# A list scheduler that plans a port: new instruction spacings, the SBUF port of VectorE and GpSimd as a resource, and new stream priorities in a two-layer hybrid backbone

## The chip, the cores and the metric

The kernel runs on one core of a Trainium2 chip. The metric is the device time of one execution in microseconds; the runs of a kernel are told by their median.

## The reference

The model takes 512 latent tokens of 1024 channels and 256 context tokens and runs two layers. Each is an RMSNorm with a learned modulation, a mixer, and a gated residual. The first layer mixes by a convolution of 31 taps and by windowed attention with 16 query heads over 4 key heads; the second by a convolution of 3 taps between gates.

```python
# layer 0
h = xn @ w_in
a = conformer_conv(h[..., :D_CONV], h[..., D_CONV:EV_Q], ...)   # GLU, 31 taps, layer norm, SiLU
q, k = axial_rope(...), axial_rope(...)
att = latent_window_attention(q, k, v, kc, vc, ev_sink[e])      # window of +-128 tokens, 256 context keys, a sink
y = (concatenate([a, att]) * silu(h[..., EV_G:])) @ ev_w_out[e]
x = x + gt * y
# layer 1
bg, cg, u, z = split(xn @ od_w_in[o], 4)
x = x + gt * ((bg * depthwise_conv(cg * u, conv_w, conv_b) * silu(z)) @ w_out)
# end
return rms_norm(x, final_g)
```

All operands are float32. The kernel multiplies each as a high and a low part, three matmuls for one.

## The kernel before

The code does not issue its instructions as it meets them. It records them in a `Plan` (`add`, line 219), gives each a rough duration (`cost`, line 266), and `schedule` (line 311) then orders them by a list schedule: it walks through a modelled time, and whichever engine is free first takes, of its instructions whose operands are ready, the one with the smallest priority number. `issue` (line 441) hands them to the engines in order of their modelled start. That order is fixed in the program; on the chip each engine works through its own list and waits by semaphore for others. As everything is issued in `issue`, nearly all rows of the profile name line 445; one goes by the names of the tiles.

A priority is the place in which an instruction was recorded plus the bias of its stream: `FILL_BIAS` for the eight input projections of the convolution, `Q_BIAS` for queries, `GATE_BIAS` for gates, `CONV_BIAS` for the taps, `ADA_BIAS` for the second layer's modulation, and so on. An instruction becomes ready when its operands' modelled ends plus a spacing from `LATENCY` (line 77, by the two engines) have passed. Some work can go to either of two engines, and `release`, within `schedule`, chooses the one that would end it earlier, with a handicap in ns: `SHY` for VectorE against GpSimd on splits, gates and additions (the engine called `F`), and `NORM_SHY` for ScalarE against VectorE on the normalisation of a row of probabilities (tile p). `LOOK` and `SOON` let a long instruction wait for a more urgent one that will soon be ready; `SWAP_COST` keeps ScalarE from changing its function table too readily.

What the groups of instructions are, by tile:
- Startup: VectorE multiplies rows of the modulation weights by the condition and sums them (junk in silb and ada, 128x1024); GpSimd makes low parts (wsl, xl); TensorE gathers keys, first queries and values.
- Attention, for each of 4 groups of heads and 4 blocks of 128 queries: scores s on TensorE, row maxima mx, the exponent's bias nm and the sink es on VectorE, exponentials p on ScalarE with their sum den, den's reciprocal, p scaled by it on ScalarE or VectorE, p transposed on TensorE (pt), split into th (ScalarE) and tl (VectorE), and the product with the values (po).
- Convolution, next to the attention: six of eight tiles on VectorE, 30 multiply-adds each into a PSUM accumulator (cv); two tiles as products on ScalarE (pr) and sums on GpSimd (cp).
- Weights: each chunk is loaded by SyncE, its high part is made on ScalarE (names ending in h), its low part on GpSimd or VectorE (l).
- The layer norm over channels (tiles u, lnq, lnrdg and others), the output projection (pya, pyb), the second layer's input (x, sq, yh, yl), sixteen blocks of four projections (pcg, pu, pbg, pz), and the last projection (f).

Of the kernel before, what the change touches and what calls it, by code (L numbers as in the profile page):

```python
# [37 lines left out]
SHY = {"DVE": 3000.0}  # L38
HI_SHY = {"POOL": 1000.0}
NORM_SHY = {"ACT": -500.0}  # L40
HI_TAGS = ()
LOOK = 0.2
SOON = 50
SWAP_COST = 800
K1_BIAS = 3.5
Q_BIAS = (0, 2.5, 3.5, 4.5)
FILL_BIAS = (-1, -1, 1, 2, 3, 4, 5, 6)
GATE_BIAS = (4.5, 6.5, 8.5, 10, 10)
# [13 lines left out]
CONV_BIAS = 20  # L62
# [5 lines left out]
for _n, _w in (("g0", 8), ("g1", 8), ("sh0", 8), ("sc0", 8), ("gt0", 8),  # L68
# [8 lines left out]
LATENCY = {"PE": {"*": 196, "PE": 0}, "ACT": {"*": 142, "PE": 271, "POOL": 170}, "DVE": {"*": 128, "PE": 300, "POOL": 155},  # L77
           "POOL": {"*": 130, "PE": 309}, "SP": {"*": 0}}
# [3 lines left out]
class Phases:  # L82
    """Memory that one phase of the kernel after another cuts into tiles of its own."""
# [17 lines left out]
class LTile:  # L101
    """A tile that is allocated when the first instruction that touches it is issued."""
# [24 lines left out]
class View:  # L127
# [12 lines left out]
    def cut(self, n):  # L140
        """free columns (n w) seen as n rows of w."""
        return View(self.t, self.chain + [lambda x: x.rearrange("p (h d) -> p h d", h=n)], self.p0, self.p1,
                    self.ix.reshape(n, -1), self.dtype)
# [17 lines left out]
class Op:  # L161
    __slots__ = ("eng", "dur", "fn", "a", "k", "prio", "deps", "tiles", "succ", "need", "ready", "aset", "seq", "start", "end", "nbytes", "alts", "shy")


class Plan:
    """Records instructions, orders them per engine by a list schedule over rough instruction costs, and
    issues them in that order."""
# [20 lines left out]
    def either(self, *engines):  # L188
        """an engine that is chosen when the operands are ready, by what each has to do until then."""
        plan = self  # L190

        class Rec:
            def __getattr__(self, m):
                return lambda *a, **k: plan.add(engines, m, {n: getattr(x, m) for n, x in engines}, a, k)

        return Rec()

    def pick(self, shy, *forms):
        """one of several (engine, its object, method, arguments, keywords) with the same operands."""
        e, x, m, a, k = forms[0]  # L200
        op = self.add("*", m, None, a, k, forms)
        op.shy = shy
        return op
# [8 lines left out]
    @contextmanager  # L212
    def after(self, *ops):
        """what the block records is ordered behind these instructions."""
        old, self.extra = self.extra, self.extra + list(ops)
        yield
        self.extra = old

    def add(self, eng, m, fn, a, k, forms=None):
# [26 lines left out]
        if isinstance(eng, tuple):  # L246
            op.alts = {}
            for n, _ in eng:
                op.eng = n
                self.cost(op, m, out, outs, a, k)  # L250
                op.alts[n] = (op.dur, fn[n], a, k, None)
            op.eng = "*"
            op.shy = self.shy
        elif forms:
            op.alts = {}
            for n, x, m, a, k in forms:
                op.eng = n
                self.cost(op, m, out, outs, a, k)
                op.alts[n] = (op.dur, getattr(x, m), a, k, op.aset)
            op.eng, op.aset = "*", None  # L260
        else:
            self.cost(op, m, out, outs, a, k)
# [3 lines left out]
    def cost(self, op, m, out, outs, a, k):  # L266
        if op.eng == "SP":
            v = out if isinstance(out, View) else k["in_"]
            op.nbytes = v.n * 4 * (v.p1 - v.p0)
            op.dur = 60  # L270
            return
# [5 lines left out]
        if op.eng == "PE":  # L277
            rhs = k.get("rhs")
            if m == "transpose":
                op.dur = n * 2 / 2.4  # L280
            elif rhs is not None and rhs.dtype == F32R:
                op.dur = n / 2.4 * (1 if n >= 256 else 4)
            elif rhs is not None and rhs.dtype == BF16:
                op.dur = n / 2.4
            else:
                op.dur = max(4 * n / 2.4, COLUMN)
# [24 lines left out]
    def schedule(self):  # L311
# [4 lines left out]
        dma_free, aset = 0.0, None  # L316

        def release(op):
            if op.alts:
# [7 lines left out]
                op.dur, op.fn, op.a, op.k, op.aset = best[2]  # L327
# [11 lines left out]
        while len(order) < total:  # L339
# [16 lines left out]
            pick, back = None, []  # L356
            while avail[e]:
# [15 lines left out]
                if e == "ACT" and op.aset and op.aset != aset and pick is None and avail[e]:  # L373
                    # another table: let ready work that needs no change go first unless this is far ahead
# [5 lines left out]
                    break  # L380
                pick = op
                break
            if pick is None and back:
                pick = self.ops[back.pop(0)[1]]
# [4 lines left out]
            if pick.dur > 300 and pend[e]:  # L389
                # a more urgent instruction that is ready in a moment goes first  # L390
# [15 lines left out]
            for t in op.tiles:  # L406
                if t not in alloc:
# [3 lines left out]
                    for pr, s in waiting.pop(t.key, []):  # L411
                        heapq.heappush(pend[self.ops[s].eng], (now, pr, s))
            op.start = now
            free[e] = now + dur
            op.end = now + dur
            if e == "SP":
                dma_free = max(dma_free, now + 1000) + op.nbytes / 360.0
                op.end = dma_free + 1000
            order.append(op)
            for t in op.tiles:  # L420
                t.left -= 1
                t.free_at = max(t.free_at, op.end)
                if not t.left:
# [6 lines left out]
                    for pr, s in more:  # L430
                        heapq.heappush(pend[self.ops[s].eng], (t.free_at + 200, pr, s))
            lat = LATENCY[e]
            for s in op.succ:
                s.need -= 1
                s.ready = max(s.ready, op.end + lat.get(s.eng, lat["*"]))
# [13 lines left out]
def backbone_kernel(ctx, tc, x_d, ctx_d, xT_d, c_d, cols_d, ada0_d, ada1_d, ws_d, wi0_d, woa_d, woc_d, wi1_d, wo1_d,  # L449
# [18 lines left out]
    # three banks: values at first, scores next, then accumulators of one bank each  # L468
# [54 lines left out]
    # mlo keeps key >= query, mhi keeps key <= query  # L523
# [4 lines left out]
    # 1 + bias of the scale columns of both layers  # L528
# [16 lines left out]
    def load_w(src, name, lo_eng, tag=None):  # L545
        """a chunk's high and low parts, each as halves of 512 columns."""
# [30 lines left out]
    # row 0 of the identity without its one, as 128 zeros  # L577
    zero, some = ident[0:1].bitcast(BF16)[:, 2:2 + P], ones[0:1].bitcast(BF16)

    def clear(bank_):  # L580
        """opens the accumulation of several groups in one bank."""
# [8 lines left out]
    def rstd_bcast(sums, n, dst, name):  # L590
        """1/sqrt(mean+eps) on every partition, from means with the tokens on partitions."""
# [11 lines left out]
    def weigh(tile_, sil_, acc, junk, eng, scale=1.0):  # L603
        """acc = scale * sum over the free axis of tile_ * sil_."""
# [6 lines left out]
    # ================= layer 0 =================  # L611
# [17 lines left out]
    def normed(t, name):  # L629
        """a block of tokens (on partitions) over its root mean square."""  # L630
# [20 lines left out]
    # keys, the first queries and the values accumulate while the modulation of each input tile arrives  # L651
# [25 lines left out]
    def modulated(k, e, src):  # L677
        """an input tile, its channels on partitions."""
# [80 lines left out]
    # keys: rows 0:64 and 64:128 both hold the head, high parts in KH, low parts in KL  # L759
    KH, KL, KC = [None] * NKV, [None] * NKV, [None] * NKV  # L760

    def twice(out, h, src):
        """(high, low) parts of one head's rows of src; the rows that hold it, and the others."""
# [23 lines left out]
    def query(pq, name):  # L787
        """the rotated queries of two heads: even head as [high; low] rows, odd head as [low; high]."""
# [19 lines left out]
    # values: per key block and head [high | low]  # L808
# [21 lines left out]
    # sigmoid(v) = (1 + tanh(v/2))/2, its half within the weights of the taps  # L830
# [19 lines left out]
    def conv_run(j, u):  # L850
        """the last POOL_TAPS[j] taps as products and sums of two more engines, the others on the vector engine."""
# [27 lines left out]
    zh, zl = [None] * NJ, [None] * NJ  # L879

    def gated(src, sg, name, tag, eng):
        """(high, low) parts of src*sg."""
# [8 lines left out]
    def attend(g, Q):  # L891
        # half the output: the gate that multiplies it is v (1 + tanh(v/2)), twice silu(v)
        att[g] = unit("A", f"att{g}", F32, (P, 2, S))
        for i in range(NT):
# [7 lines left out]
            for t in range(2):  # L902
                # two heads side by side in three banks: [local | context] and [context | local]
# [133 lines left out]
    # The mean of seven of the eight tiles is taken off all, so that what is left of the whole mean is found with the  # L1037
    # squares: its own square is an eighth of theirs at most.
# [67 lines left out]
    # the convolution half goes by input tiles over all banks, halves of the tokens in banks of their own; the  # L1106
    # last two tiles are taken for one half first
# [19 lines left out]
    # tail of the projection and the modulated input of layer 1, for one half of the tokens after the other  # L1127
# [43 lines left out]
    def turn(blocks):  # L1171
        """the stream with its tokens on partitions, for the last residual."""
# [13 lines left out]
    # ================= layer 1 =================  # L1186
# [53 lines left out]
    # gate of layer 1 on every partition, and the last norm's weight  # L1240
# [17 lines left out]
    # parts of it: half of the channels of a block of tokens, and a quarter at the very end  # L1258
    ss = new((P, 3 * NT), F32, "ss", "ss", 1)
    V.memset(ss, 0.0)  # L1260
    for hf in range(2):
# [13 lines left out]
        # the last input tiles of the second half go one part after the other  # L1275
# [98 lines left out]
```

## Time and profile before

| | us |
|---|---|
| median of 3 runs | 1038.64 |
| lowest and highest | 1036.52, 1039.46 |
| span of the profiled execution, first to last instruction | 1035.6 |
| TensorE busy in the span | 960.7 |
| VectorE busy | 704.1 |
| ScalarE busy | 499.9 |
| GpSimd busy | 437.7 |

The profiled execution has no time of its own beside its span; the difference of the median to the span, 3.0 us, stands for what lies around it. A matmul is pipelined, its end is modelled, and so TensorE's busy time is not TensorE at its peak.

### The profile page before, as it was taken

The page shows a single profiled execution, that of the slowest core. Times are in us where ns is not written, and L with a number is a line of the kernel's source. Part 1 is how long each engine was busy: PE and PEld are TensorE (multiplying, and loading weights), DVE is VectorE, ACT ScalarE, POOL GpSimd, SP SyncE. Part 2 cuts the span into 40 slices and gives each one's busy share as a digit, 9 for nine tenths or more (in the row PEclk, how much of TensorE's full clock was granted, in tenths as well). Part 3 has the DMA queues.
Part 4 walks back from the last instruction along what each step waited for, and adds up shares of the span by engine and source line. Part 5 has one row for each costly group of instructions (what it writes and reads, how often), then busy time and mean ns, then how long its engine had stood idle before and what let it go on. Part 6 is the DMA issues. An engine that isn't in the chain of part 4 may idle for free.

```text
span 1035.6 us, 13212 instructions
## 1 busy us (share of the span) xinstructions
PE 960.7 (93%) x4804; PEld 787.8 (76%) x4804; DVE 704.1 (68%) x1094; ACT 499.9 (48%) x938; POOL 437.7 (42%) x359
## 2 busy tenths in 40 slices
PE   5779989999997989998879899999999999999997
PEld 2667767778775767876679898888888888888886
DVE  5997499999999999888843847644444444453343
ACT  5435889778876874452434523233232332323232
POOL 5988777744676678877776500000000000000011
PEclk9899999999999999998989899999999999999999
DMA  7542210211113325442244125422222232222222
GB/s 296 170 173 73 73 59 21 82 41 41 41 41 104 116 86 180 165 164 102 82 143 162 62 101 184 142 86 99 102 97 87 102 103 84 99 102 82 102 82 81
DMA packets 31460, 109.07 MB, mean 105 GB/s; under 512 B 3490, under 2 KB 3618, under 8 KB 31396
## 3 DMA queue, kind: packets, MB, share of 16 engines
q1 hardware_dynamic: 31396, 108.24, 29.9%
q8 instruction: 37, 0.61, 0.2%
q14 instruction: 27, 0.22, 0.1%
HBM read 106.13 MB, written 2.10 MB: 105 GB/s over the span
## 4 chain that ended last, share of the span: by engine, by line
PE 62%; DVE 27%; ACT 6%; issue 3%; POOL 2%; POOLq 0%; ACTq 0%; DVEq 0%
PE pz L445 8%; PE pbg L445 8%; PE pu L445 8%; PE pcg L445 8%; PE f L445 8%; DVE cv L445 5%; PE pya L445 4%; DVE p L445 3%; DVE silb L445 2%; PE pg L445 2%; PE pyb L445 2%; DVE tl L445 2%; PE s L445 2%; PE pt L445 2%; PE po L445 2%
## 5 line engine op out<-in xcount | busy, mean ns | idle before, releaser
L445 POOL TENSOR_TENSOR x1t<-x1t,fg 128x512 f32<-128x512 f32 x4 | 6.4, 1626 | 394.3 <-ACT fy L445 394.3
L445 DVE SCALAR_TENSOR_TENSOR cv<-u,cols,cv 128x512 f32<-128x512 f32 x180 | 135.2, 751 | 12.7 <-ACT cv L445 8.9
L445 POOL TENSOR_TENSOR cp<-cp,pr 128x512 f32<-128x512 f32 x60 | 79.7, 1329 | 13.6 <-ACT pr L445 11.6
L445 PE MATMUL pt<-ident,p 128*128 128x128 f32 x288 | 55.4, 282 | 18.4 <-DVE p L445 8.5
L445 PEld LDWEIGHTS pt<-ident,p 128*128 128x128 f32 x288 | 36.6, 141 | 37.7 <-DVE p L445 12.5
L445 ACT ACTIVATE th<-pt 128x512 fp32r<-128x512 f32 x72 | 41.3, 597 | 23.5 <-PE pt L445 22.8
L445 ACT ACTIVATE p<-s,nm 128x512 f32<-128x512 f32 (+1 forms) x64 | 46.8, 737 | 8.6 <-DVE nm L445 8.4
L445 DVE TENSOR_TENSOR tl<-pt,th 128x512 fp32r<-128x512 f32 x72 | 47.4, 682 | 3.4 <-ACT th L445 3.2
L445 DVE TENSOR_REDUCE mx<-s 128x2 f32<-128x1024 f32 (+1 forms) x32 | 43.2, 1350 | 4.5 <-PE s L445 4.4
L445 ACT ACTIVATE pr<-u,cols 128x512 f32<-128x512 f32 x60 | 41.2, 715 | 2.4 <-POOL cp L445 2.2
L445 PE MATMUL po<-tl,vv 128*128 128x512 f32 x72 | 32.1, 446 | 2.4 <-DVE tl L445 2.4
L445 DVE TENSOR_SCALAR p<-p,den 128x512 f32<-128x512 f32 (+1 forms) x34 | 33.2, 1009 | 0.6
L445 ACT ACTIVATE xf<-tp,mab 128x512 f32<-128x512 f32 (+1 forms) x16 | 10.7, 669 | 43.0 <-DVE mab L445 38.5
L445 PE MATMUL po<-th,vv 128*128 128x512 f32 x72 | 29.4, 408 | 0.0
L445 ACT ACTIVATE p<-p,den 128x640 f32<-128x640 f32 (+1 forms) x30 | 21.9, 773 | 8.4 <-DVE den L445 8.0
L445 DVE SCALAR_TENSOR_TENSOR ac<-ac,silc 128x1024 f32<-128x1024 f32 x6 | 10.7, 1790 | 21.8 <-DMA ac<-in_ada_dram 21.8
L445 DVE SCALAR_TENSOR_TENSOR silb<-ada,silb 128x1024 f32<-128x1024 f32 x16 | 24.7, 1546 | 0.2
L445 DVE SCALAR_TENSOR_TENSOR ya<-cu,cols,ya 128x512 f32<-128x512 f32 x32 | 23.9, 748 | 0.6
L445 PEld LDWEIGHTS po<-tl,vv 128*128 128x128 f32 x72 | 13.9, 193 | 7.0 <-DVE tl L445 5.3
L445 DVE TENSOR_TENSOR ya<-pbg,ya 128x512 f32<-128x512 f32 x16 | 11.0, 690 | 11.8 <-PE pbg L445 11.8
L445 POOL TENSOR_TENSOR xl<-xf,xh 128x512 fp32r<-128x512 f32 x8 | 17.0, 2125 | 2.9 <-ACT xh L445 2.9
L445 DVE TENSOR_TENSOR z1l<-ya,z1h 128x512 fp32r<-128x512 f32 x16 | 11.1, 692 | 10.5 <-ACT z1h L445 10.5
(1669 smaller groups left out, 3517.0 us busy)
## 6 DMA issues: line engine op xcount, KB each, us to landing
ada<-in_ada_dram SPq DMA_DIRECT2D x16, 512.0 KB, 4.2
wicg<-in_wi_dram SPq DMA_DIRECT2D x16, 512.0 KB, 3.2
wiu<-in_wi_dram SPq DMA_DIRECT2D x16, 512.0 KB, 3.2
wibg<-in_wi_dram SPq DMA_DIRECT2D x16, 512.0 KB, 3.2
wiz<-in_wi_dram SPq DMA_DIRECT2D x16, 512.0 KB, 3.2
wf<-in_wo_dram SPq DMA_DIRECT2D x16, 512.0 KB, 3.3
wb<-in_wi_dram SPq DMA_DIRECT2D x8, 512.0 KB, 3.3
wa<-in_wi_dram SPq DMA_DIRECT2D x8, 512.0 KB, 3.3
```

The source lines that it names most:

```text
L445: op.a = op.fn(*a, **k)
```

## The change

The recorded arithmetic stays the same. The scheduler gets other numbers and one rule more:
- Matmul costs gain a fixed part (512 columns: 227 instead of 213 ns), and the spacings between engines are replaced by a lag of the engine that ends (`LAG`) and a hop to the one that starts (`HOP`).
- `cost` marks an instruction with `port` if it is GpSimd's (but for memset) or one of VectorE's with its operands in SBUF. `schedule` keeps the time at which the port comes free. An instruction with the mark starts in the model when the port is free, and holds it for its duration. VectorE passes over up to 6 such instructions while the port is taken for over 60 ns more, and takes another that is ready; if that would last longer than the port's remaining time, the first that was passed over goes after all.
- A tile's memory is believed free 60 instead of 200 ns after its last use.
- `SHY`, `NORM_SHY`, `LOOK`, `SOON`, `SWAP_COST` and some biases have new values.

The diff, without its removed comments and docstrings:

```diff
-SHY = {"DVE": 3000.0}
-NORM_SHY = {"ACT": -500.0}
+SHY = {'DVE': 4267.0}
+NORM_SHY = {'ACT': -1961.0}
-LOOK = 0.2
-SOON = 50
-SWAP_COST = 800
+LOOK = 0.7
+SOON = 44.37
+HELD = 0
+SWAP_COST = 1443.63
-Q_BIAS = (0, 2.5, 3.5, 4.5)
-FILL_BIAS = (-1, -1, 1, 2, 3, 4, 5, 6)
-GATE_BIAS = (4.5, 6.5, 8.5, 10, 10)
+Q_BIAS = (0, 2.5, 3.66, 4.5)
+FILL_BIAS = (0.69, -2.96, 1, 2, 3, 4, 5, 6)
+GATE_BIAS = (4.5, 6.5, 8.5, 10, 11.57)
-CONV_BIAS = 20
+CONV_BIAS = 20.81
-LATENCY = {"PE": {"*": 196, "PE": 0}, "ACT": {"*": 142, "PE": 271, "POOL": 170}, "DVE": {"*": 128, "PE": 300, "POOL": 155},
-           "POOL": {"*": 130, "PE": 309}, "SP": {"*": 0}}
+LAG = {"PE": 165, "ACT": 100, "DVE": 84, "POOL": 56, "SP": 0}
+HOP = {"PE": 56, "ACT": 35, "DVE": 35, "POOL": 78, "SP": 60}
...
     def cost(self, op, m, out, outs, a, k):
+        sb = lambda v: hasattr(v, "shape") and not (isinstance(v, View) and v.t.psum) or isinstance(v, View) and not v.t.psum
+        op.port = op.eng == "POOL" and m != "memset"
+        if op.eng == "DVE":
+            if m == "tensor_tensor":
+                op.port = sb(a[1]) and sb(a[2])
+            elif m == "scalar_tensor_tensor":
+                op.port = sb(a[1]) and sb(a[3])
+            elif m in ("tensor_scalar", "tensor_copy"):
+                op.port = sb(a[1]) and sb(a[0])
...
-                op.dur = n * 2 / 2.4
+                op.dur = 110
             elif rhs is not None and rhs.dtype == F32R:
-                op.dur = n / 2.4 * (1 if n >= 256 else 4)
+                op.dur = (n + 32) / 2.4 if n >= 256 else 110
             elif rhs is not None and rhs.dtype == BF16:
-                op.dur = n / 2.4
+                op.dur = max(54, n / 2.4 + 6)
             else:
-                op.dur = max(4 * n / 2.4, COLUMN)
+                op.dur = max(4 * n / 2.4 + 12, 224)
...
+                if op.port and port > now + 60 and e == "DVE" and len(held) < 6:
+                    held.append((pr, s))
+                    continue
                 pick = op
                 break
+            if held and (pick is None or pick.dur > port - now + HELD):
+                if pick is not None:
+                    heapq.heappush(avail[e], (pick.prio, pick.seq))
+                pick = self.ops[held.pop(0)[1]]
+            for x in held:
+                heapq.heappush(avail[e], x)
...
+            if op.port:
+                now = max(now, port)
+                port = now + dur
             op.start = now
             free[e] = now + dur
-            op.end = now + dur
+            op.end = now + dur + LAG[e]
             if e == "SP":
                 dma_free = max(dma_free, now + 1000) + op.nbytes / 360.0
-                op.end = dma_free + 1000
+                op.end = dma_free + 1000 - 60
...
-                        heapq.heappush(pend[self.ops[s].eng], (t.free_at + 200, pr, s))
-            lat = LATENCY[e]
+                        heapq.heappush(pend[self.ops[s].eng], (t.free_at + 60, pr, s))
...
-                s.ready = max(s.ready, op.end + lat.get(s.eng, lat["*"]))
+                s.ready = max(s.ready, op.start + dur if e == "PE" and s.eng == "PE" else op.end + HOP.get(s.eng, 50))
```

## Rows read from the trace of the kernel before

**Rows 1.** The page's head line.

```profile
span 1035.6 us, 13212 instructions
```

**Rows 2.** Windows by stage: us, busy (instructions) of PE, PEld, DVE, ACT, POOL; PEclk, DMA share, GB/s.

```profile
0.00:104.00 104.00, 76.78 (x379) 60.12 (x380) 84.95 (x135) 50.27 (x108) 83.25 (x69) 0.93 0.50 179
104.00:415.00 311.00, 286.57 (x1488) 224.24 (x1487) 283.26 (x424) 239.03 (x461) 213.16 (x179) 0.98 0.21 74
415.00:466.00 51.00, 51.00 (x224) 41.45 (x223) 42.99 (x52) 26.01 (x44) 42.01 (x31) 1.00 0.47 165
466.00:622.00 156.00, 140.14 (x890) 126.74 (x889) 102.16 (x177) 60.88 (x114) 89.75 (x71) 0.92 0.31 109
622.00:984.00 362.00, 362.00 (x1591) 297.14 (x1590) 169.73 (x276) 109.09 (x182) 1.99 (x2) 1.00 0.31 105
984.00:1036.00 52.00, 44.21 (x240) 38.13 (x238) 21.04 (x35) 14.64 (x31) 7.55 (x11) 0.96 0.23 81
```

**Rows 3.** The chain that ended last, a projection of layer 1: start, us.

```profile
630.43 5.49 PE pcg L445 x24
```

**Rows 4.** The chain within 104 to 415 us, shares by line.

```profile
by line: DVE p L445 8.9%; DVE cv L445 8.5%; PE pg L445 7.0%; DVE tl L445 6.1%; PE s L445 6.1%; PE pt L445 6.0%; PE po L445 5.9%; DVE mx L445 5.8%; PE pq L445 4.8%; issue 3.5%; PE ag L445 3.4%; DVE nm L445 3.3%; DVE den L445 3.0%; DVE att L4
```

**Rows 5.** VectorE's timeline, at 162 and 246 us: start, us.

```profile
162.27 0.15 DVE L445 TENSOR_TENSOR den<-den,es 128x4 f32<-128x4 f32 x1
...
162.67 0.55 DVE L445 TENSOR_SCALAR p<-p,den 128x640 f32<-128x640 f32 x1
...
246.38 0.49 DVE L445 TENSOR_SCALAR p<-p,den 128x512 f32<-128x512 f32 x1
```

**Rows 6.** VectorE by groups, 104 to 415 us: busy us, mean ns, idle before.

```profile
L445 DVE SCALAR_TENSOR_TENSOR cv<-u,cols,cv 128x512 f32<-128x512 f32 x115 | 86.3, 750 | 4.1 <-ACT cv L445 2.1
...
L445 DVE TENSOR_SCALAR p<-p,den 128x640 f32<-128x640 f32 x16 | 17.6, 1128 | 0.3
L445 DVE SCALAR_TENSOR_TENSOR nm<-mx,nsink 128x2 f32<-128x2 f32 x32 | 16.1, 503 | 0.8
L445 DVE TENSOR_SCALAR p<-p,den 128x512 f32<-128x512 f32 x18 | 15.6, 903 | 0.3
...
L445 DVE TENSOR_TENSOR es<-nm,cols 128x4 f32<-128x4 f32 x16 | 11.1, 696 | 0.4
L445 DVE SCALAR_TENSOR_TENSOR ag<-ag,silc 128x1024 f32<-128x1024 f32 x6 | 9.9, 1655 | 0.0
L445 DVE TENSOR_TENSOR den<-den,es 128x4 f32<-128x4 f32 x16 | 7.9, 495 | 2.0 <-ACT es L445 1.8
```

**Rows 7.** VectorE's timeline, at 43 us and from 331 us.

```profile
43.00 2.18 DVE L445 SCALAR_TENSOR_TENSOR silb<-ada,silb 128x1024 f32<-128x1024 f32 x1
...
331.08 1.22 DVE L445 TENSOR_TENSOR es<-nm,cols 128x4 f32<-128x4 f32 x1
332.22 1.21 DVE L445 SCALAR_TENSOR_TENSOR ag<-ag,silc 128x1024 f32<-128x1024 f32 x1
...
333.37 1.24 DVE L445 TENSOR_TENSOR den<-den,es 128x4 f32<-128x4 f32 x1
```

**Rows 8.** GpSimd's timeline, 330 to 336 us.

```profile
330.50 1.78 POOL L445 TENSOR_TENSOR cp<-cp,pr 128x512 f32<-128x512 f32 x1
333.14 1.45 POOL L445 TENSOR_TENSOR wa7l<-wa,wa7h 128x512 fp32r<-128x512 f32 x1 [0.86 <-ACT wa7h L445]
...
334.64 1.26 POOL L445 TENSOR_TENSOR cp<-cp,pr 128x512 f32<-128x512 f32 x1
```

**Rows 9.** ScalarE by groups, 104 to 415 us.

```profile
L445 ACT ACTIVATE p<-p,den 128x640 f32<-128x640 f32 x16 | 12.4, 823 | 2.5 <-DVE den L445 2.3
```

**Rows 10.** VectorE by groups, 466 to 530 us.

```profile
L445 DVE TENSOR_SCALAR lnrdg<-ident,lnrs 128x128 f32<-128x128 f32 x4 | 3.8, 996 | 0.3 <-POOL lnrs L445 0.3
...
L445 DVE TENSOR_SCALAR lnbdg<-ident,lnmx 128x128 f32<-128x128 f32 x4 | 0.9, 273 | 0.0
```

**Rows 11.** TensorE's waits, 466 to 622 us: total, times, longest us.

```profile
PE pyb L445 <- DVE x L445: 7.2, 2, 6.8
```

More of the change, by code (lines that the diff above doesn't have):

```diff
@@ L37 @@
 ADA_POOL = ((1, 5), (1, 3, 5, 7), (1, 5))
-SHY = {"DVE": 3000.0}
-HI_SHY = {"POOL": 1000.0}
-NORM_SHY = {"ACT": -500.0}
+SHY = {'DVE': 4267.0}
+HI_SHY = {'POOL': 1000.0}
+NORM_SHY = {'ACT': -1961.0}
 HI_TAGS = ()
-LOOK = 0.2
-SOON = 50
-SWAP_COST = 800
+LOOK = 0.7
+SOON = 44.37
+HELD = 0
+SWAP_COST = 1443.63
 K1_BIAS = 3.5
-Q_BIAS = (0, 2.5, 3.5, 4.5)
-FILL_BIAS = (-1, -1, 1, 2, 3, 4, 5, 6)
-GATE_BIAS = (4.5, 6.5, 8.5, 10, 10)
+Q_BIAS = (0, 2.5, 3.66, 4.5)
+FILL_BIAS = (0.69, -2.96, 1, 2, 3, 4, 5, 6)
+GATE_BIAS = (4.5, 6.5, 8.5, 10, 11.57)
 ADA_BIAS = 15
@@ L161 @@
 class Op:
-    __slots__ = ("eng", "dur", "fn", "a", "k", "prio", "deps", "tiles", "succ", "need", "ready", "aset", "seq", "start", "end", "nbytes", "alts", "shy")
+    __slots__ = ("eng", "dur", "fn", "a", "k", "prio", "deps", "tiles", "succ", "need", "ready", "aset", "seq", "start", "end", "nbytes", "alts", "shy", "port")
 class Plan:
@@ L250, in add @@
                 self.cost(op, m, out, outs, a, k)
-                op.alts[n] = (op.dur, fn[n], a, k, None)
+                op.alts[n] = (op.dur, fn[n], a, k, None, op.port)
             op.eng = "*"
@@ L258, in add @@
                 self.cost(op, m, out, outs, a, k)
-                op.alts[n] = (op.dur, getattr(x, m), a, k, op.aset)
+                op.alts[n] = (op.dur, getattr(x, m), a, k, op.aset, op.port)
             op.eng, op.aset = "*", None
@@ L315, in schedule @@
         used, turn, waiting, alloc = {}, {}, {}, set()
-        dma_free, aset = 0.0, None
+        dma_free, aset, port = 0.0, None, 0.0
         def release(op):
@@ L326, in release @@
                 op.eng = best[1]
-                op.dur, op.fn, op.a, op.k, op.aset = best[2]
+                op.dur, op.fn, op.a, op.k, op.aset, op.port = best[2]
             heapq.heappush(pend[op.eng], (op.ready, op.prio, op.seq))
@@ L355, in schedule @@
                 heapq.heappush(avail[e], (pr, s))
-            pick, back = None, []
+            pick, back, held = None, [], []
             while avail[e]:
```

## The prediction

> **What bounds the kernel now.** I read the page first for the span, then busy times by stage, then the chain of waits of the stage that has most idle time, then VectorE's groups of instructions in that stage, and last single rows of its timeline beside GpSimd's.
>
> The profiled execution spans 1035.6 us [rows 1]; the median of the runs is 1038.64, so 3.0 us lie around the span, and I add them at the end. By stage [rows 2], the reader is to see four different limits:
> - 622 to 984 us: TensorE is busy for 362.00 of 362.00 us. One projection of 24 matmuls takes 5.49 us [rows 3], 229 ns each. An order of instructions can give nothing here. In the last 52 us 7.8 us are idle, nearly all of it the tail behind the last matmul.
> - 415 to 466 us: TensorE is busy for 51.00 of 51.00 us.
> - 104 to 415 us (attention, convolution, gates): TensorE is busy for 286.57 of 311 us, so 24.4 us are idle; VectorE is busy for 283.26, that is 91%, GpSimd for 213.16. The chain of waits here runs through VectorE's p, cv, tl, mx, nm, den before any matmul but pg [rows 4]. VectorE is the bound, with TensorE close behind.
> - 466 to 622 us (layer norm, output projection, start of layer 1): TensorE is idle for 156 − 140.14 = 15.9 us, and the mean granted clock is 0.92: for about a sixth of the time it stood at the lower of its two levels, 1.2 GHz.
> - 0 to 104 us: TensorE is idle for 27.2 us; VectorE and GpSimd are each busy for about 84 us of it.
>
> Busy time on VectorE is not all work. A sum of 128x4 elements (den) takes 0.15 us when nothing disturbs it [rows 5] and 495 ns in the mean [rows 6]. The timeline shows why: es of 128x4 takes 1.22 us while GpSimd's cp is under way and ends as that ends (330.50 + 1.78 = 332.28); den takes 1.24 us while GpSimd's wa7l runs, and ends at 334.6 as that does [rows 7, 8]. In the startup a weighing of 128x1024 takes 2.18 us; one that meets nothing takes 1.21 [rows 7]. One of the two engines stands still while the other holds something that both need for operands in SBUF. The cv instructions, whose accumulator is in PSUM, do not show it: 750 ns in the mean over 115 [rows 6].
>
> **How much VectorE loses so, 104 to 415 us.** Mean less undisturbed, times count [rows 5, 6]: p of 640 columns 16 × (1128 − 550) = 9.2 us; p of 512 columns 18 × (903 − 490) = 7.4; nm, taken at den's price, 32 × (503 − 150) = 11.3; es 16 × (696 − 150) = 8.7; den 16 × (495 − 150) = 5.5; ag 6 × (1655 − 1210) = 2.7, with 1.21 us from [rows 7]. Sum 44.8 us over 104 instructions, 14% of the stage.
>
> **The change part by part.** The instructions stay what they are, but for the choices between engines; no load or matmul is added. What moves is the order on each engine, and which engine does the work that may go either way.
>
> *Spacings and TensorE costs.* The old cost of a 512-column matmul is 512/2.4 = 213 ns, the new one 544/2.4 = 227; the trace has 229 [rows 3]. The old plan thus believes each projection 0.37 us shorter than it is (24 × 15.4 ns). Spacings from VectorE to TensorE fall from 300 to 84 + 56 = 140 ns. A truer plan puts fewer instructions ahead of operands that are late; it removes no work. I price it at nothing by itself, since it has no row of its own: above by TensorE's 24.4 us of idle time, below by the same stretch's waits getting worse, which I put at 8 us, a third of it.
>
> *The port in the plan.* VectorE now passes over an instruction with SBUF operands if the modelled port is taken for over 60 ns more, and runs another ready one, unless that is longer than the time left. The candidates are cv (750 ns measured) and tl. A GpSimd sum of 128x512 takes 1.26 us undisturbed [rows 8], in the plan 1225 ns; a cv is planned at 663. The rule can act only while 663 of 1225 ns are still to come, in 46% of the cases if the arrivals are spread evenly. Then a cv of 0.75 us runs in what was a stall. Ceiling: 104 × 0.46 × 0.75 = 36 us of VectorE's time. That needs the chip's GpSimd to be where the plan has it. Nothing holds the phase but the semaphores, so I take a third: 12 us. Ends: 0 and 36.
>
> *More normalisation on ScalarE.* The head start of ScalarE for p goes from 500 to 1961 ns. VectorE now does 34 of the 64, at about 1 us each in the mean [rows 6]; ScalarE does its share at 823 ns for 640 columns [rows 9]. I take 12 moved: 12 us off VectorE, 10 us onto ScalarE, which is idle for 311 − 239.03 = 72 us of the stage [rows 2], though there it also stands before each exponential. Ends: 0 and 34 us. The handicap of VectorE for split and gate work (3000 to 4267) acts the same way, unseen; I put it at nothing within these ends, GpSimd's 98 us of idle time being its cover.
>
> *What the span gets.* VectorE is relieved of 24 us. TensorE, next in line, has only 24.4 us of idle time, and VectorE is not last at every step, so I pass on half: **−12 us**. Ends: −24.4, all the idle time, and +8 as above.
>
> *466 to 622 us.* The layer norm's steps meet the same stall: lnrdg takes 996 ns where lnbdg, the same operation and shape, takes 273, so 4 × 0.72 = 2.9 us [rows 10]. TensorE's longest wait is 6.8 us for VectorE's x, 7.2 in total [rows 11]; on VectorE a weighing (ac) and the splits of the next weights stand in that queue. A planner that counts the port can put these elsewhere; I take a third of the 15.9 us of idle time: **−5 us**. Ends: −15.9 and +5.
>
> *0 to 104 us.* VectorE's work here is weighings, with two operands in SBUF [rows 7], and GpSimd's is splits. The rule finds nothing else to run, so the two go on in turns: **0**. Ends: −4 (some splits, 1.26 us on GpSimd like cp, go to VectorE, where a subtraction like tl is planned at 602 ns) and +3.
>
> *After 622 us*: **0**. *LOOK, SOON, SWAP_COST and the new stream priorities* decide who goes first among ready work; LOOK 0.7 lets an engine stand idle for up to 0.7 of an instruction for a more urgent one. No row prices them; they lie within the ends above.
>
> Sum: −12 − 5 = −17; 1035.6 − 17 + 3.0 = 1021.6, say **1022 us**.
>
> **The rivals.**
> *Phase lost.* On the chip the lock falls to whoever comes first, and that isn't where the plan has it: the low clock between 466 and 622 us alone is not in the plan. Passing over an instruction is then a random swap. What stays is the moved p, half of 12 us, and a truer TensorE cost: about −6 − 2 = −8, 1031 us. For it: a static order can't answer to an engine that is late; against it: the semaphores tie the engines together every few microseconds. The Trainium skill, "SBUF — State Buffer", section "Who interferes with whom", says that whoever issues first gets the shared pair for the whole instruction and the other fully blocks, and that "Issue order, not op shape, decides who blocks"; this speaks against fixing it in a plan, and by it the sum would be that of this rival. The trace agrees with the full block (den waits to the end of wa7l).
> *All idle time comes back.* If VectorE's 44.8 us fall by most of the 36, TensorE becomes the bound in both stages: 1035.6 − 24.4 − 15.9 + 3 = 998 us. Against it: that leaves not one wait of TensorE.
> *Slower: urgent short instructions held.* nm, es and den are what the exponentials and p wait for: 32 + 16 + 16 = 64. Passed over for one cv where the port is in fact free, each comes 0.75 us later: 64 × 0.46 × 0.75 = 22 us on the attention chain; half of it is filled by other work, the moved p give back 3 to 4: +8, 1047 us. It decides once over about half of the held ones would have found the port free. For it: nm and den alone make up 6.3% of the stage's chain [rows 4]; against it: their means, three to five times the undisturbed time [rows 5, 6], say that they often do meet a taken port.
> *No change.* The order differs, the pacing remains: 1035.5 to 1041.8.
>
> **How the numbers follow.** A difference of 0.3% (3.1 us) is about what a measurement of this kernel can tell from none. Chances: forecast 0.42 (its own range 1010 to 1028), phase lost 0.18, all idle time back 0.14, no change 0.10, slower 0.16. Faster: 0.42 + 0.18 + 0.14 = 0.74. The range 1003 to 1043 leaves out about half of the third case below and two thirds of the slower case above, 0.18 together.
>
> **What the profile of the changed kernel would show.** The means of nm, es, den and p on VectorE between 104 us and the end of attention fall towards 0.15 and 0.5 us; p on VectorE falls from 34 to about 22; TensorE's idle time before the first full stretch falls by about 12 us; from the first projection of layer 1 on nothing changes but the start; the startup ends at about the same time. I am wrong if the means fall and the span does not (then VectorE's stalls were cover for something else), if they don't fall (phase lost), or if the exponentials wait longer for nm.

## The result, and the profile after

The changed kernel takes 1019.51 us in the median of 4 runs (1018.87 to 1021.25), against 1038.48 for the kernel before. The ratio is 0.9828 [0.9811, 0.9846]: 1.7% faster. The forecast was 1022 us. The profiled execution took 1019.0 us with a span of 1017.2, 18.4 us less than before [rows 1].

The windows by stage of the changed kernel, columns as in [rows 2]; the last one is left out, as the span ends within it:

```profile
0.00:104.00 104.00, 75.81 (x367) 58.91 (x368) 84.55 (x132) 48.91 (x103) 76.34 (x69) 0.92 0.48 174
104.00:415.00 311.00, 300.34 (x1583) 237.13 (x1582) 261.17 (x406) 258.69 (x497) 223.57 (x183) 1.00 0.25 84
415.00:466.00 51.00, 50.29 (x219) 40.41 (x218) 45.62 (x61) 23.52 (x40) 46.33 (x33) 1.00 0.48 160
466.00:622.00 156.00, 140.42 (x893) 126.99 (x892) 102.27 (x183) 62.09 (x115) 87.09 (x71) 0.91 0.35 115
622.00:984.00 362.00, 362.00 (x1608) 298.01 (x1607) 167.10 (x269) 111.20 (x188) 6.43 (x4) 1.00 0.30 101
```

Only the second row differs in what matters. Between 104 and 415 us TensorE's idle time falls from 24.4 to 10.7 us, VectorE's busy time from 283.26 to 261.17, ScalarE's rises from 239.03 to 258.69. The windows have fixed bounds, and the work in them shifts; so the reader should also look at when certain instructions start. From TensorE's timeline after (start us, us) come the last product with the values and the first product with the layer norm's output, and from the chain that ended last the first projection of layer 1 over 512 columns:

```profile
379.25 0.39 PE L470 MATMUL po<-tl,vv 128*128 128x512 f32 x1
...
507.56 0.58 PE L470 MATMUL pya<-z0h,woc0h 128*128 128x256 f32 x1 [4.17 <-ACT z0h L470]
```

```profile
590.07 5.49 PE pcg L470 x24
```

The first two are at 396.07 and 524.73 in the trace of before, the same piece of the chain (pcg x24) at 608.46. So the attention ends 16.8 us earlier, the layer norm delivers 17.2 us earlier, layer 1 runs 18.4 us earlier, and so does the end. Nearly all of the gain is made before 380 us. Not all of it is idle time that went: up to layer 1 TensorE's idle time, startup included, falls from 67.5 to 55.1 us, and its busy time for the same matmuls from 540.8 to 534.8; the granted clock between 104 and 415 us is 0.98 before and 1.00 after.

VectorE's groups between 104 and 415 us, columns as in [rows 6]:

```profile
L470 DVE SCALAR_TENSOR_TENSOR cv<-u,cols,cv 128x512 f32<-128x512 f32 x112 | 83.9, 749 | 4.3 <-ACT cv L470 2.8
...
L470 DVE SCALAR_TENSOR_TENSOR nm<-mx,nsink 128x2 f32<-128x2 f32 x32 | 13.5, 423 | 0.8
...
L470 DVE TENSOR_SCALAR p<-p,den 128x640 f32<-128x640 f32 x7 | 9.0, 1281 | 0.1
L470 DVE SCALAR_TENSOR_TENSOR ag<-ag,silc 128x1024 f32<-128x1024 f32 x6 | 8.7, 1448 | 0.0
L470 DVE TENSOR_TENSOR es<-nm,cols 128x4 f32<-128x4 f32 x16 | 6.9, 428 | 0.2
L470 DVE TENSOR_TENSOR den<-den,es 128x4 f32<-128x4 f32 x16 | 6.6, 411 | 2.8 <-ACT es L470 2.7
L470 DVE TENSOR_SCALAR p<-p,den 128x512 f32<-128x512 f32 x8 | 5.7, 714 | 0.1
```

p on VectorE falls from 34 to 15. The means of nm, es, den and ag fall from 503, 696, 495 and 1655 ns to 423, 428, 411 and 1448, far from the 150 ns (1210 for ag) of an undisturbed one [rows 5, 7]. By the prediction's formula the loss to port waits is now 7 × 0.73 + 8 × 0.22 + 32 × 0.27 + 16 × 0.28 + 16 × 0.26 + 6 × 0.24 = 25.6 us, for 44.8 before; 9.7 of the 19.2 saved belong to p, most of it because there are fewer of them.

### The profile page after: what moved, and what is told of

Its sections match the earlier page's. It is cut to its first block, busy times and chain, and to the rows that moved or that the text cites. A ratio compares the mean times of both kernels' runs of the same rounds, so it can differ in the third digit from the quotient of the medians.

```text
span 1017.2 us, 13188 instructions
## 1 busy us (share of the span) xinstructions
PE 954.7 (94%) x4804; PEld 783.6 (77%) x4804; DVE 672.1 (66%) x1069; ACT 511.5 (50%) x957; POOL 442.9 (44%) x365
## 4 chain that ended last, share of the span: by engine, by line
PE 49%; POOL 2%; DVE 1%; issue 0%; ACT 0%; POOLq 0%; DVEq 0%; ACTq 0%
PE pbg L470 9%; PE pz L470 9%; PE pcg L470 9%; PE pu L470 9%; PE f L470 8%; PE pya L470 3%; PE pyb L470 2%; POOL u L470 1%; POOL sq L470 0%; POOL w L470 0%; PE lnb L470 0%; PE gt L470 0%; DVE x1t L470 0%; POOL rs_0sd L470 0%; POOL z0l L470 0%
## 5 line engine op out<-in xcount | busy, mean ns | idle before, releaser
L470 PE MATMUL pt<-ident,p 128*128 128x128 f32 x288 | 48.3, 274 | 1.4 <-DVE q_0rr L470 0.5
L470 ACT ACTIVATE th<-pt 128x512 fp32r<-128x512 f32 x72 | 41.6, 598 | 12.3 <-PE pt L470 11.3
L470 ACT ACTIVATE p<-p,den 128x640 f32<-128x640 f32 (+1 forms) x49 | 34.4, 768 | 0.7 <-DVE den L470 0.5
L470 DVE SCALAR_TENSOR_TENSOR silb<-ada,silb 128x1024 f32<-128x1024 f32 x16 | 25.6, 1600 | 0.3
L470 DVE SCALAR_TENSOR_TENSOR ya<-cu,cols,ya 128x512 f32<-128x512 f32 x32 | 24.1, 752 | 1.1
L470 DVE SCALAR_TENSOR_TENSOR ada<-ada,silb 128x1024 f32<-128x1024 f32 x15 | 21.5, 1463 | 0.0
L470 ACT ACTIVATE xf<-tp,mab 128x512 f32<-128x512 f32 (+1 forms) x16 | 10.7, 669 | 20.1 <-DVE mab L470 14.0
L470 PEld LDWEIGHTS po<-th,vv 128*128 128x128 f32 x72 | 13.5, 187 | 8.9 <-ACT th L470 6.4
L470 DVE TENSOR_TENSOR ya<-pbg,ya 128x512 f32<-128x512 f32 x16 | 11.1, 691 | 12.4 <-PE pbg L470 12.2
L470 PE MATMUL tp<-ident,xt 128*128 128x128 f32 x32 | 7.3, 354 | 11.0 <-ACT xf L470 6.0
```

What stands on the lines that cost most here:

```text
L470: op.a = op.fn(*a, **k)
```

## The experiments

A run of the kernel before stands beside every one, on the same chip; the ratios are to it. First come eight kernels in which a number or a rule of the planner differs, so that it makes a new order; then four in which the order is kept and one thing in it is moved. A trace is one execution. Beside these experiments single executions of the kernel before took 1030.4 to 1040.3 us, and the traced ones of two kernels (rounded, no passing over) lie 3 to 4 us above their medians; so a difference of 2 or 3 us between two traces says little.

**The head start of the normalisation taken back.**

```diff
-NORM_SHY = {'ACT': -1961.0}
+NORM_SHY = {'ACT': -500.0}
```

> The changed kernel with ScalarE's head start for the normalisation set back from 1961 to 500 ns, all else new. Theory M (VectorE relieved in the attention: fewer p, fewer port stalls): p on VectorE goes back from 15 towards 30, VectorE gets some 12 us more work between 104 and 415 us, half of it reaches the end: 1024 to 1028 us. Rival P (the new stream priorities do it): within 3 us of 1019.5.

Measured: 1033.34 us, ratio 0.9989 [0.9965, 1.0013]. p on VectorE is back at 33, as theory M had it, but the whole gain is gone, which is more than either theory had.

**The port taken out of the plan.**

```diff
-        op.port = op.eng == "POOL" and m != "memset"
-        if op.eng == "DVE":
+        op.port = False
+        if False:
```

> The changed kernel with no instruction marked for the port, so that neither the model's waits nor the passing over remain; spacings and all numbers new. Theory M: the means of nm, es and den go back to those of before (0.5, 0.7, 0.5 us) and 6 to 9 us are lost: 1025 to 1029 us. Rival (phase lost: the plan of the port is a random swap on the chip): means as in the changed kernel, time within 3 us of 1019.5.

Measured: 1046.39 us, ratio 1.0116 [1.0071, 1.0162]; slower than the kernel before. VectorE's groups from 104 to 415 us of this run, columns as above:

```profile
L470 DVE SCALAR_TENSOR_TENSOR nm<-mx,nsink 128x2 f32<-128x2 f32 x32 | 17.9, 558 | 0.9
...
L470 DVE TENSOR_TENSOR es<-nm,cols 128x4 f32<-128x4 f32 x16 | 11.0, 690 | 0.5
...
L470 DVE TENSOR_TENSOR den<-den,es 128x4 f32<-128x4 f32 x16 | 7.5, 468 | 2.1 <-ACT es L470 1.9
```

The means are back at those of before, as theory M had it; the loss against the changed kernel, 1.0116/0.9828 = 1.029 or 30 us, is over three times what it had.

**The new scheduler with all old numbers.** SHY, NORM_SHY, LOOK, SOON, SWAP_COST and the four biases as before; spacings, costs and port new.

> The new scheduler (spacings, costs, port) with all the old numbers: handicaps, LOOK, SOON, SWAP_COST and stream biases. Theory M: the port's half stays, the normalisation's half goes: 1026 to 1031 us. Rival P: nearly all goes, 1034 to 1040 us.

Measured: 1042.32 us, ratio 1.0072 [1.0046, 1.0097]; worse than both theories. TensorE's longest wait is for the low part of a weight of the output projection (woc0l), of which GpSimd makes the second half only at 535.70 us, behind the layer norm's products; the changed kernel has both halves by 488 us. From TensorE's waits, 500 to 600 us:

```profile
PE pya L470 <- POOL woc0l L470: 15.3, 1, 15.3
```

**The old scheduler with all new numbers.**

> The old scheduler (spacings, costs, no port) with all the new numbers. Theory M: the normalisation's half comes, the port's doesn't: 1027 to 1032 us. Rival P: nearly all comes, 1018 to 1024 us. A third theory (numbers suit only the scheduler that they were set for): no faster than before, 1036 us or more.

Measured: 1052.50 us, ratio 1.0177 [1.0131, 1.0222]: the third theory's side. The numbers alone, without the scheduler that they were set for, cost 18 us.

Each half of the change loses and the whole gains, so the parts can't be added. Either they need each other, or any new order is a throw of dice. The next four ask which.

**Four numbers rounded.**

```diff
-SHY = {'DVE': 4267.0}
-NORM_SHY = {'ACT': -1961.0}
-SOON = 44.37
-SWAP_COST = 1443.63
+SHY = {'DVE': 4300.0}
+NORM_SHY = {'ACT': -2000.0}
+SOON = 50
+SWAP_COST = 1500.0
```

> The changed kernel with four numbers rounded: SOON 50, SWAP_COST 1500, handicaps 4300 and 2000 ns. Theory M3 (the parts of the change belong together, but the numbers need not be exact): within 5 us of 1019.5. Theory R (the order is rugged: any small change of a number moves the end by some 10 us, and the changed kernel is a chosen low point): 1026 us or more.

Measured: 1042.57 us, ratio 1.0062 [1.0040, 1.0085]: theory R. Up to the first transposition of p, at 126.4 us, every engine has the instructions of the changed kernel in the same order, TensorE's and VectorE's within 0.14 us. One place of the loss is plain to see; the next four fences are rows of this run's timelines of TensorE, ScalarE, GpSimd and VectorE, in this order:

```profile
393.29 1.70 PE L470 MATMUL pt<-ident,p 128*128 128x128 f32 x4 [9.08 <-ACT p L470]
```

```profile
391.48 1.06 ACT L470 ACTIVATE ag<-ag 128x1024 f32<-128x1024 f32 x1 [1.92 <-POOL ag L470]
392.44 0.18 ACT L470 ACTIVATION_READ_ACCUMULATOR ag<-ag 128x1 f32 x1
392.53 1.93 ACT L470 ACTIVATE p<-p,den 128x512 f32<-128x512 f32 x3
```

```profile
389.11 2.34 POOL L470 TENSOR_TENSOR ag<-ag,silc 128x1024 f32<-128x1024 f32 x1 [1.20 <-DMA ag<-in_ada_dram]
```

```profile
389.59 1.87 DVE L470 TENSOR_TENSOR den<-den,es 128x4 f32<-128x4 f32 x1 [0.21 <-ACT es L470]
```

A weighing for the gate of layer 0's residual (ag), which only the sums behind the output projection need, sits on GpSimd when the sum den comes, and den waits for its end (389.11 + 2.34 = 391.45). ScalarE's half of that weighing stands ahead of p in ScalarE's list, and holds p until 392.5. By then TensorE has no projection left to fill with: the last convolution input began its last matmuls at 331 us, where the changed kernel's did at 341, and TensorE stands for 9.08 us. The two delays make up about 2.5 of these (1.87 − 0.15 us of den, and 392.5 − 391.7 of p, as den's reciprocal ends at 391.7); the rest is the way from scores to probabilities, which nothing covers. In the whole stretch from there to the end of the attention it is idle for 14.4 us, for 0.4 in the changed kernel. The passing over is in force here too, and still es and den wait about as long as before the change; VectorE's groups from 104 to 415 us of this run:

```profile
L470 DVE TENSOR_TENSOR den<-den,es 128x4 f32<-128x4 f32 x16 | 10.4, 652 | 2.5 <-ACT es L470 2.5
L470 DVE TENSOR_TENSOR es<-nm,cols 128x4 f32<-128x4 f32 x16 | 9.9, 620 | 0.2
```

**No passing over.**

```diff
-                if op.port and port > now + 60 and e == "DVE" and len(held) < 6:
+                if False:
```

> The changed kernel without the passing over; the model still makes a port instruction wait and hold the port, so the plan's times and choices of engine count it. If the passing over is what pays, nm, es and den go back to 0.5 to 0.7 us and the time comes near that of the run without the port, 1040 us or more; if it is the counting in the plan, within 5 us of 1019.5.

Measured: 1043.98 us, ratio 1.0078 [1.0051, 1.0104]: the first side, by the time and by the means. VectorE's groups from 104 to 415 us:

```profile
L470 DVE SCALAR_TENSOR_TENSOR cv<-u,cols,cv 128x512 f32<-128x512 f32 x87 | 65.4, 751 | 1.5
...
L470 DVE SCALAR_TENSOR_TENSOR nm<-mx,nsink 128x2 f32<-128x2 f32 x32 | 20.6, 645 | 1.0
...
L470 DVE TENSOR_TENSOR es<-nm,cols 128x4 f32<-128x4 f32 x16 | 10.7, 670 | 0.4
L470 DVE TENSOR_SCALAR p<-p,den 128x640 f32<-128x640 f32 x8 | 10.1, 1257 | 0.3
L470 DVE TENSOR_TENSOR den<-den,es 128x4 f32<-128x4 f32 x16 | 8.5, 531 | 4.7 <-ACT es L470 4.7
...
L470 DVE TENSOR_SCALAR p<-p,den 128x512 f32<-128x512 f32 x8 | 8.0, 1001 | 0.3
```

nm, es, den and p take 57.9 us for 41.7 in the changed kernel, and cv gets 65.4 us for 83.9: 87 multiply-adds in this window for 112. The waits cost TensorE little in the attention (table below). They are paid later: all 30 multiply-adds of the last convolution tile, 24 of them in one row, are left for the time after 492 us, and the layer norm's sum, and TensorE with it, waits for them. TensorE's longest wait from 440 to 540 us, and VectorE's timeline:

```profile
PE lnq L470 <- DVE u L470: 30.6, 1, 30.6
```

```profile
492.07 18.95 DVE L470 SCALAR_TENSOR_TENSOR cv<-u,cols,cv 128x512 f32<-128x512 f32 x24
```

**Spacings and TensorE costs alone** (old numbers, no port; the 60 ns after a tile's last use stay with them).

> The old numbers and no port, only the new spacings and TensorE costs, against the kernel before. Theory M (they remove no work): within 5 us of before, 1033 to 1043 us. If a truer plan is worth something by itself: under 1030 us.

Measured: 1061.40 us, ratio 1.0248 [1.0216, 1.0280]. Outside both: truer spacings by themselves gave the slowest kernel of all.

**The head start alone, in the old scheduler.**

> The kernel before with ScalarE's head start for the normalisation set to 1961 ns alone. Theory M: p on VectorE 34 to about 15, VectorE relieved of 19 us between 104 and 415 us, half of it to the end: 1026 to 1031 us. Theory R: anything from 1025 to 1050 us, with the attention shorter and a later stage longer.

Measured: 1049.21 us, ratio 1.0127 [1.0091, 1.0162]: theory R by the time, but not its stages: the attention is not shorter, its last product with the values comes at 401.8 us for 396.1 before; from there to layer 1 it is 7.0 us longer.

What the ten orders have in common shows when TensorE's idle time is taken by stretches instead of from the end. Each number is the length of a window less TensorE's busy time in it; the windows end at the first transposition of p, the last matmul of a convolution input, the last product with the values, and the first 512-column projection of layer 1.

| order | port in the plan | pt to last convolution input | to the end of attention | to layer 1 |
|---|---|---|---|---|
| changed kernel | yes | 6.7 | 0.4 | 17.7 |
| head start back | yes | 3.6 | 8.6 | 24.8 |
| old numbers | yes | 5.9 | 10.8 | 25.5 |
| rounded | yes | 4.6 | 14.4 | 24.1 |
| no passing over | yes | 2.3 | 9.0 | 38.7 |
| before | no | 16.8 | 5.1 | 15.9 |
| no port | no | 17.1 | 4.3 | 21.5 |
| new numbers only | no | 11.3 | 3.2 | 39.5 |
| spacings only | no | 22.1 | 4.9 | 25.1 |
| head start only | no | 15.2 | 7.0 | 27.2 |

The windows of the changed kernel, of before and of the rounded one, for the first of these columns:

```profile
126.50:341.00 214.50, 207.83 (x1129) 163.20 (x1128) 179.51 (x289) 185.49 (x363) 146.71 (x124) 1.00 0.18 60
```

```profile
130.50:361.60 231.10, 214.28 (x1149) 167.65 (x1148) 218.24 (x332) 184.89 (x360) 151.26 (x127) 0.99 0.17 59
```

```profile
126.40:331.30 204.90, 200.30 (x1069) 156.48 (x1068) 167.04 (x260) 177.18 (x342) 149.71 (x127) 1.00 0.17 56
```

Every order that counts the port is idle for 2.3 to 6.7 us in the first stretch, every one that doesn't for 11.3 to 22.1. The passing over isn't needed for that in an order planned without it. But TensorE then runs through its projections sooner: the last convolution input ends at 330 to 333 us in the other four orders that count the port, at 341 in the changed kernel, at 347 to 368 in those that don't. Without filler while the last heads finish, it gives the time back there, and more in the layer norm: 33 to 48 us of idle time in those four (last two columns together), 18 us in the changed kernel. Part of that has one cause: with the head start back, the old numbers and the rounded ones, TensorE waits 8.3, 15.3 and 12.8 us for a low part of woc that GpSimd makes behind the layer norm's products, where the changed kernel has these parts before them. The changed kernel is the one order that keeps what it gained.

The startup splits the ten another way. The first transposition of p comes at 124.9 to 127.5 us in the six orders that have the new SHY, LOOK, SOON, SWAP_COST and stream priorities (rounded or not), at 130.5 to 134.5 in the four that have the old ones. The head start, the spacings and the port do not split them so. What these numbers do behind the startup was never measured apart.

The last four kernels keep an order and move one thing, so that no new throw is made.

**The passed ones put back.** In the changed kernel's order every instruction that was passed over is issued ahead of the first that passed it.

```diff
+            passed += [(x[1], op.seq) for x in held if x[1] != op.seq]
...
+        for h, p in first.items():
+            key[h] = min(key[h], (self.ops[p].start, 0, h))
+        return sorted(order, key=lambda o: key[o.seq])
```

> The changed kernel's order, kept as it was planned, but each of the 68 VectorE instructions that were passed over is put back in front of the first instruction that passed it. No new plan is made, so the roughness of the planner is out. If the passing over pays on the chip: nm, es, den and the weighings (26 of the 68) wait more, and 6 us or more are lost, 1025 us or more. If it is the counting of the port in the plan that pays: within 4 us of 1019.5.

Measured: 1039.79 us (1034.62 to 1040.13), ratio 1.0028 [1.0004, 1.0051]; against the changed kernel 1.0028/0.9828 = 1.020, 21 us. VectorE's groups from 104 to 415 us:

```profile
L477 DVE SCALAR_TENSOR_TENSOR nm<-mx,nsink 128x2 f32<-128x2 f32 x32 | 18.1, 565 | 0.8
...
L477 DVE TENSOR_SCALAR p<-p,den 128x640 f32<-128x640 f32 x7 | 10.1, 1438 | 0.2
...
L477 DVE TENSOR_SCALAR p<-p,den 128x512 f32<-128x512 f32 x8 | 7.2, 894 | 0.3
L477 DVE TENSOR_TENSOR den<-den,es 128x4 f32<-128x4 f32 x16 | 6.7, 420 | 3.7 <-ACT es L477 3.6
L477 DVE TENSOR_TENSOR es<-nm,cols 128x4 f32<-128x4 f32 x16 | 6.3, 392 | 0.4
```

The first side. nm waits 142 ns more each, p 0.16 to 0.18 us, den and es no more than in the changed kernel; these are 32 × 0.14 + 17.3 − 14.7 = 7 us. The traced execution spans 17.3 us more than the changed kernel's: the first transposition of p comes 3.6 us later, the last convolution input 10.4, the end of the attention 12.3, layer 1 17.3. So more is lost than the longer waits of nm and p. The order was planned with the passing, and what stands behind the instructions put back comes late with them; how much of the rest that is, no run shows.

**The normalisations on the engines of before, in the changed kernel's order.**

```diff
     order = plan.schedule()
+    for op, e in zip([o for o in plan.ops if o.alts and "ACT" in o.alts and "DVE" in o.alts], NORMS):
+        op.eng = {"D": "DVE", "A": "ACT"}[e]
+        op.fn, op.a, op.k = op.alts[op.eng][1:4]
```

> The changed kernel's order kept, but the 64 normalisations on the engines of before: 26 go back from ScalarE to VectorE, 7 the other way, at the same places of the order. VectorE has 19 more of about 1 us. Theory M: half reaches the end, 1026 to 1032 us. If VectorE no longer bounds the attention: within 3 us of 1019.5.

Measured: 1034.11 us, ratio 0.9976 [0.9958, 0.9995]; against the changed kernel 0.9976/0.9828 = 1.015, 15 us. Theory M's direction, above its range: four fifths instead of half of the 19 us.

**The same the other way, in the order of before.** The edit is the same, with the changed kernel's engines.

> The order of the kernel before kept, but the 64 normalisations on the engines of the changed kernel (15 on VectorE for 34). Theory M: half of 19 us reaches the end, 1026 to 1031 us. If the order must be planned for it: within 4 us of before.

Measured: 1028.20 us, ratio 0.9921 [0.9894, 0.9949]; 8 us less than before, theory M. Planned anew with the same head start, it had been a loss of 13 us.

**The layer norm's closing work on VectorE.**

```diff
+    for op in plan.ops[ln0:ln1]:
+        if op.alts and op.eng == "POOL":
+            op.eng = "DVE"
+            op.fn, op.a, op.k = op.alts["DVE"][1:4]
```

> The changed kernel's order kept, but the layer norm's closing products, gates and low parts (u, zl) that stood on GpSimd go to VectorE at the same places. They take turns at the port on both engines, and one takes 1.28 us on GpSimd and 0.69 on VectorE when alone. If the exclusive port bounds this stage, the first product z0 is there 3 to 4 us earlier and the low clock shortens too: 1011 to 1017 us. If VectorE's own queue then bounds it: 1018 to 1025 us.

Measured: 1018.99 us, ratio 0.9834 [0.9803, 0.9864]; no difference from the changed kernel, so the second side by the time. The changed kernel's timelines show the two engines taking turns (VectorE, then GpSimd), and in this run VectorE alone:

```profile
498.68 2.37 DVE L470 TENSOR_TENSOR u<-u,lnbs 128x512 f32<-128x512 f32 x2 [0.35 <-ACT lnbs L470]
500.96 3.25 DVE L470 TENSOR_TENSOR u<-u,lnrs 128x512 f32<-128x512 f32 x2
```

```profile
498.72 3.27 POOL L470 TENSOR_TENSOR u<-u,lnbs 128x512 f32<-128x512 f32 x2 [1.30 <-ACT lnbs L470]
501.95 3.21 POOL L470 TENSOR_TENSOR u<-u,lnrs 128x512 f32<-128x512 f32 x2
```

```profile
500.93 2.50 DVE L470 TENSOR_TENSOR u<-u,lnbs 128x512 f32<-128x512 f32 x4 [0.35 <-ACT lnbs L470]
503.34 2.49 DVE L470 TENSOR_TENSOR u<-u,lnrs 128x512 f32<-128x512 f32 x4
```

Eight products take 505.16 − 498.68 = 6.5 us in turns and 505.83 − 500.93 = 4.9 alone, 0.61 us each. But the kept order has all eight ahead of the first gate, and TensorE's wait for z0 is 4.2 us in both runs. This run's stretch began 2.2 us later, so that z0 is ready at the same time. The step is shorter and the end is not.

TensorE's idle time in the four kept orders, by the stretches of the table above:

| kept order | pt to last convolution input | to the end of attention | to layer 1 |
|---|---|---|---|
| changed kernel, passed ones put back | 10.3 | 1.6 | 20.7 |
| changed kernel, normalisations as before | 12.8 | 2.8 | 17.9 |
| before, normalisations as changed | 12.4 | 3.2 | 15.2 |
| changed kernel, layer norm's work on VectorE | 6.6 | 0.4 | 19.0 |

The first two were planned with the port and are as idle in the first stretch as orders without it. The short idle time there thus belongs to a plan that counts the port and is carried out as planned, not to the counting alone.

## Why the prediction was right

The time was right within 2.5 us, and so was the place of most of it. Part of that closeness is luck: the attention gave 16.8 us for the 12 forecast, all behind it 1.6 for 5, and the two errors nearly cancel. The 3.0 us added for what lies around the span are about 1.8 in every execution on record beside it (1019.0 − 1017.2 here); the rest is that the traced execution of before was faster than the median. Step by step:

*VectorE bounds the attention, TensorE close behind.* Right. VectorE's busy time in the stage fell by 22.1 us (24 forecast), TensorE's idle time by 13.7 (12 forecast), and the attention ended 16.8 us earlier, 4.0 of these by the first transposition of p.

*More normalisation on ScalarE, 12 of 34 moved.* The mechanism was right, the size too small: 19 moved, and VectorE's time on p fell from 33.2 to 14.7 us. With orders kept, this is worth 8 us in the order of before and 15 in that of after. Beside the 21 us of the passed ones put back, these are more than the whole gain, so neither is a share of it.

*The port in the plan, 12 us of VectorE's time.* The port waits other than p's fell by 9.5 us. That VectorE works multiply-adds off in what were stalls is borne out: planned anew without the passing over, nm, es, den and p take 16.2 us more and cv 18.5 less, and putting the passed instructions back in the kept order costs 21 us, more than its waits. That TensorE's idle time in the attention falls by it was only half right: planned anew without it, the first stretch is idle for 2.3 us, and the price comes behind the attention, as the wait of 30.6.

*Spacings and TensorE costs at nothing, ends of 24.4 and 8 us.* Alone, in a new plan, they cost 26 us, outside the lower end. What was mis-sized is the term, "a third" of the idle time: the price of a new order that happens to be bad isn't bounded by idle time that the old one has.

*466 to 622 us, −5 us.* Wrong. From the end of the attention to layer 1 the changed kernel gains 18.4 − 16.8 = 1.6 us, and its idle time there is 17.7 us for 15.9. The wait for x is gone, and others took its place: 5.5 us for a low part woa5l on GpSimd, 4.2 for z0h.

*Startup 0, and the new stream priorities within the ends.* The last transposition of inputs comes 4 us later than before, the first of p 4 us earlier. Those 4 us go with SHY, LOOK, SOON, SWAP_COST and the stream priorities, which the prediction had left without a price.

*The rivals.* Phase lost doesn't hold for this order: es and nm did fall, and undoing the passing lengthened nm. As a rule it isn't refuted: in the rounded order, with the same passing over, es and den take 620 and 652 ns. Its own sum (−6 − 2) also pays 2 us for truer TensorE costs that the forecast puts at nothing; no row shows them. All idle time back didn't happen: 10.7 us are left in the attention. The slower case, urgent instructions held, isn't in the changed kernel: between 104 and 415 us ScalarE's exponentials wait for nm for 7.7 us, for 8.4 before. The prediction missed the largest matter, that the order is rough: four rounded numbers turn −1.7% into +0.6%. Of the eight other orders planned here seven are slower than before and one ties with it. The chance of 0.16 for slower was that of this change as it stands; no row of the trace of before could have shown which neighbour it was. That the changed kernel stands at such a low point is luck as far as the forecast goes. Why just this order doesn't give its gain back, I can't say beyond its rows: it has no wait of TensorE over 5.5 us after the startup's end, and it has the low parts of woc in time.

## What to carry to other kernels

Take TensorE's idle time by stretches that end at instructions, not from the total: a rule of the planner that works in every order that has it can be invisible in the end time, because filler runs out earlier and the next stretch gives the time back. In a static order, work that comes late on an in-order queue left TensorE standing for 15 us (one low part of a weight) and 31 us (one convolution tile). So judge an edit to a planner with the order kept (move one thing in it), and don't credit or blame the edit for the new order that it happens to throw. A kept order has a price of its own, as it wasn't planned for what is moved: 21 us where the waits grew by 7. Where two engines take turns at a port, as in the layer norm here, they do not work side by side; send work that needs no port (ScalarE here) before balancing the two.

## What was not expected of the hardware

A sum of 4 columns on VectorE, 0.15 us of work, waits for the end of a GpSimd instruction: den took 1.87 us behind a weighing of 2.34. The smaller the instruction, the larger its share of waiting: it is about two thirds of the time of nm, es and den even in the changed kernel. On VectorE a chain of 128x512 products takes 0.61 us each without GpSimd beside it and 1.6 in turns with it, so that for these eight products VectorE alone (4.9 us) is faster than both engines together (6.5).
